# Two output tiles in the attention and a three-tile ring for pre-split weights in a hybrid encoder layer

## The chip, the cores and the metric

The kernel runs on one core of a Trainium2 chip. Its time is that of one execution on the device, in microseconds (us): a median of 1939.59 us over three runs (1938.0 to 1943.59). One further execution was recorded by the hardware profiler; all rows below come from that one.

## The reference, cut to what matters

One layer of an encoder is applied to two sequences, a prompt of 1024 tokens and a sample of 256, each with 16 meta tokens ahead, all in float32.

```
a = rms_norm(h);  p = a @ w_in                    # c_q, c_kv, k_rope and the Hyena input u
s = (q_nope @ k_nope.T + q_rope @ k_rope.T) * scale   # 4 heads, no mask
o_attn = softmax(s) @ v
o_hy   = two gated long convolutions of u (by FFT)
mix = concat(rms_norm(o_attn), rms_norm(o_hy)) @ w_o
h = h + rms_norm(mix)
m = square(relu(rms_norm(h) @ w_ff1)) @ w_ff2     # 1024 -> 4096 -> 1024
h = h + rms_norm(m)
```

## The kernel before

Each float32 product is made of three faster ones (`mm3`, lines 261 to 263): both factors are split into a rounded high part and the rest, the low part. For a weight piece (128 x 512, 256 KB) the high part is a cast on ACT (line 269) and the low part a subtraction, mostly on POOL (line 272); `ring` (line 391) does this for each piece that is streamed.

Phase B computes the attention. It runs over 40 units, 4 heads by 10 tiles of 128 queries: 8 tiles of the prompt and 2 of the sample. In the last head the two sample tiles come first, so units 30 and 31 are the sample's and 32 to 39 the prompt's. In the loop's step i, PE computes the scores of unit i (`softmax`, into the PSUM tile `sset0` or `sset1`), then transposes the probabilities of unit i-1 (`turn`: eight blocks, and a ninth at line 1032, the "last transpose" of a unit), and weights the values of a pair of units (`weigh`, line 1038, into the PSUM tile `po`). At the end of `weigh` ACT copies the transposed reciprocals of the softmax sums from PSUM to `rb` (line 1053), DVE multiplies `po` with `rb` into `ot` (line 1055), and SP's queue stores `ot` to DRAM (line 1056, `oa<-ot`). `rb` and `ot` have one tile each. The scores' ninth block holds 16 keys and 112 columns that POOL sets to zero (line 1005, `MEMSET prob`).

Beside the attention POOL prepares weights of the later sample path (`presplit`, line 363): the first 80 pieces of that path (16 of the output projection, then `w_ff1` and `w_ff2` in turn). A piece is loaded into a tile `pre_raw` (line 372), cast into `pre_hi` (line 384), the cast is subtracted in place (line 272), and the low part is stored to DRAM (line 377, `lo_w_...`). There are four tiles `pre_raw`; a load into one must wait until the store out of it has landed. The load of piece k+2 is written behind the split of piece k and the store of piece k-1. The loop calls `presplit` two times in odd steps and three times in even ones, and runs it to its end before step 33. There the convolution of the sample's Hyena part (`hyena_sample`, line 1469) begins; it loads its input `zs` (line 1478) on SP's queue, PE transposes 16 columns of each of its four parts (line 1441) and then its blocks (line 1495), and its work is woven into the remaining steps.

Later, beside the prompt's Hyena convolution, the sample's output projection and MLP run as filler (`sample_path`). For a pre-split piece `ring` loads the raw weight and the stored low part (lines 398 and 399); for others POOL subtracts (lines 406 and 272). The ring there has four tiles.

What sets the order: within a step the instructions of PE, ACT and DVE are pinned in the written order (`pin`), except the convolution's; everything else is ordered by a scheduler by priority and by its own estimate of when inputs are ready. On the chip each engine's queue and SP's DMA queue run strictly in the order that results.

Of the kernel before, what the change touches and what calls it, by code (L numbers as in the profile page):

```python
# [13 lines left out]
F32 = mybir.dt.float32  # L14
# [7 lines left out]
P = 128  # L22
# [156 lines left out]
def mk(ap, dims):  # L179
    return bass.AP(tensor=ap.tensor, offset=ap.offset, ap=[ap.ap[0]] + [list(d) for d in dims])  # L180
# [54 lines left out]
class Builder:  # L235
# [127 lines left out]
    def presplit(self, pool, n):  # L363
        nc = self.nc
        keys = list(self.sample_pieces())[:n]
        raws = {}

        def load(k):
            if k < n:
                raw = raws[k] = pool.tile([P, 512], F32, name="pre_raw", bufs=4)  # L370
                src = self.piece(*keys[k])
                nc.sync.dma_start(raw.rearrange("p (a b) -> p a b", a=4) if len(src.shape) == 3 else raw, src)

        def store(k):
            if k in raws:
                d = self.d_lo[keys[k]] = self.dr.tile([P, 512], F32, name="lo_" + "_".join(map(str, keys[k])))
                nc.sync.dma_start(d, raws.pop(k))

        load(0)
        load(1)  # L380
        yield
        for k in range(n):
            t = pool.tile([P, 512], F32R, name="pre_hi", bufs=1)
            nc.gpsimd.tensor_copy(t, raws[k])
            self.lo(raws[k], raws[k], t, nc.gpsimd)
            store(k - 1)
            load(k + 2)
            yield
        store(n - 1)
# [514 lines left out]
    def phase_b(self):  # L904
# [4 lines left out]
        with ExitStack() as st:  # L909
# [5 lines left out]
            wk = self.pool(st, "b_work", 2)  # L915
# [122 lines left out]
            def weigh(h, t, qp, pth, ptl, rcs):  # L1038
                vh, vl = t[4:]
                nb, b0 = (8, 0) if qp < 4 else (2, 8)  # L1040
                po = pv.tile([P, 512], F32, name="po", bufs=1)
                o = po[:, :256]
                for b in range(nb):
                    if b == nb // 2:
                        yield
                    self.mm3(o, vh[:, b0 + b], vl[:, b0 + b], pth[:, b], ptl[:, b], b == 0, False)
                b = 8 if qp < 4 else 10
                self.mm3(o, vh[:, b], vl[:, b], pth[:, 8], ptl[:, 8], False, True)
                for i in range(2):
                    nc.tensor.transpose(po[:, 256 + i * 128:384 + i * 128], mk(rcs[i], [[0, 128]]), self.ident)  # L1050
                yield
                rb = wk.tile([P, 256], F32, name="rb", bufs=1)
                nc.scalar.copy(rb, po[:, 256:])
                ot = wk.tile([P, 256], F32, name="ot", bufs=1)
                self.tt(ot, o, rb, ALU.mult)
                (nc.gpsimd if h >= self.dbg.get("oq", 4) else nc.sync).dma_start(self.d_oa[h][:, qp * 256:qp * 256 + 256], ot)
                yield
# [4 lines left out]
            with self.hp(4):  # L1062
                self.hi(krh[0:64], self.ka[0:64])
                self.lo(krl[0:64], self.ka[0:64], krh[0:64])
                raw, rk = stage(TM), stage(T)
                nc.sync.dma_start(rk[64:128], self.ka[0:64])
                nc.sync.dma_start(raw[64:128], self.qr[0:64])
                self.hi(krh[64:128], rk[64:128])
                self.lo(krl[64:128], rk[64:128], krh[64:128])
                self.hi(qst[0][0:64], self.qr[0:64])  # L1070
                self.hi(qst[0][64:128], raw[64:128])
                self.lo(qst[0][64:128], raw[64:128], qst[0][64:128])
                self.ropes.close()
                hps.append(self.pool(st, "b_head1"))
                pre_st = st.enter_context(ExitStack())
                pre = self.presplit(self.pool(pre_st, "b_pre"), 80)
                next(pre)
                for _ in range(self.dbg.get("n6", 6)):
                    next(prep, None)
# [20 lines left out]
            for i in range(n + 3):  # L1100
# [34 lines left out]
                if i >= 3 and i % 2 == 1:  # L1135
                    h, qt = units[i - 3]
                    weighing = weigh(h, heads[h], qt // 2, *pts.pop((i - 3) // 2))
# [781 lines left out]
```

## Time and profile before

| | |
|---|---|
| median of three runs | 1939.59 us |
| profiled execution, its own time | 1943.15 us |
| its span | 1941.4 us |
| PE busy | 1775.0 us (91%), 9806 matmuls |
| DVE busy | 1149.4 us (59%) |
| ACT busy | 751.6 us (39%) |
| POOL busy | 689.2 us (36%) |
| chain that ended last | PE 64%, DVE 15%, DMA 9%, issue 4%, POOL 4%, ACT 4% |

The chain follows the last instruction back, at each step to what released it. A line such as `x <-DMA y` after an idle time names what ended it. SPq is SP's queue of DMA issues. The attention stage lies from about 380 to 685 us, the prompt's convolution with the sample's filler from 685 to 945 us.

### The profile page before, as it was taken

The page shows a single profiled execution, that of the slowest core. Times are in us where ns is not written, and L with a number is a line of the kernel's source. Part 1 is how long each engine was busy: PE and PEld are TensorE (multiplying, and loading weights), DVE is VectorE, ACT ScalarE, POOL GpSimd, SP SyncE. Part 2 cuts the span into 40 slices and gives each one's busy share as a digit, 9 for nine tenths or more (in the row PEclk, how much of TensorE's full clock was granted, in tenths as well). Part 3 has the DMA queues.
Part 4 walks back from the last instruction along what each step waited for, and adds up shares of the span by engine and source line. Part 5 has one row for each costly group of instructions (what it writes and reads, how often), then busy time and mean ns, then how long its engine had stood idle before and what let it go on. Part 6 is the DMA issues. An engine that isn't in the chain of part 4 may idle for free.

```text
span 1941.4 us, 26719 instructions
## 1 busy us (share of the span) xinstructions
PE 1775.0 (91%) x9806; PEld 1561.1 (80%) x9806; DVE 1149.4 (59%) x1862; ACT 751.6 (39%) x1362; POOL 689.2 (36%) x660
## 2 busy tenths in 40 slices
PE   7999999887878988998899799899999999999996
PEld 6899999787778777887779678777888888888885
DVE  6588875753446868999642956763333334333347
ACT  6344443443334454332344565544322222222232
POOL 2112113377882210222376743234422222222234
PEclk9899999988999998999899899999999999999997
DMA  4454535367776276767543574345211111111104
GB/s 165 141 177 159 169 111 196 106 202 242 231 246 210 76 255 200 253 222 240 175 139 120 174 233 143 121 130 166 96 45 44 44 44 44 50 52 56 56 5 142
DMA packets 183654, 275.70 MB, mean 142 GB/s; under 512 B 15258, under 2 KB 89952, under 8 KB 183394
## 3 DMA queue, kind: packets, MB, share of 16 engines
q1 hardware_dynamic: 174936, 254.97, 40.3%
q0 software_dynamic: 5872, 17.06, 2.9%
q10 hardware_dynamic: 2714, 1.96, 0.3%
q8 instruction: 77, 1.26, 0.3%
q14 instruction: 55, 0.45, 0.1%
HBM read 210.90 MB, written 60.38 MB: 140 GB/s over the span
## 4 chain that ended last, share of the span: by engine, by line
PE 64%; DVE 15%; DMA 9%; issue 4%; POOL 4%; ACT 4%; SPq 0%; POOLq 0%; ACTq 0%; DVEq 0%
PE p L261 13%; PE p L263 13%; PE p L262 12%; PE pp L261 2%; PE pp L262 2%; PE pp L263 2%; PE ips L1685 2%; PE wps L263 2%; PE wps L261 2%; PE wps L262 2%; DVE bl L275 2%; POOL pre_raw L272 1%; PE dps L1452 1%; DMA w_raw<-in_w_ff 1%; DMA pre_raw<-in_w_ff 1%
## 5 line engine op out<-in xcount | busy, mean ns | idle before, releaser
L272 POOL TENSOR_TENSOR w_lo<-w_raw,w_hi 128x512 fp32r<-128x512 f32 x276 | 383.3, 1400 | 678.7 <-ACT w_hi L269 622.0
L269 ACT CAST w_hi<-w_raw 128x512 fp32r<-128x512 f32 x388 | 237.8, 619 | 441.4 <-PE p L262 293.3
L261 PE MATMUL p<-sh,w_hi 128*128 128x512 f32 (+1 forms) x800 | 284.5, 360 | 11.1 <-DVE acc L275 4.1
L262 PE MATMUL p<-sl,w_hi 128*128 128x512 f32 (+1 forms) x800 | 283.5, 354 | 11.7 <-DVE sl L272 11.6
L261 PE MATMUL p<-a2h,w_hi 128*128 128x512 f32 (+1 forms) x784 | 285.0, 364 | 8.5 <-ACT a2h L282 4.9
L263 PE MATMUL p<-a2h,w_lo 128*128 128x512 f32 (+1 forms) x784 | 282.7, 361 | 8.8 <-DMA w_lo<-lo_w_ff 6.8
L263 PE MATMUL p<-sh,w_lo 128*128 128x512 f32 (+1 forms) x800 | 284.1, 355 | 4.4 <-POOL w_lo L272 4.4
L262 PE MATMUL p<-a2l,w_hi 128*128 128x512 f32 (+1 forms) x784 | 281.1, 359 | 0.1
L275 DVE TENSOR_TENSOR acc<-acc,p 128x512 f32<-128x512 f32 (+1 forms) x284 | 184.8, 656 | 146.4 <-PE p L263 145.9
L261 PEld LDWEIGHTS p<-sh,w_hi 128*128 128x128 f32 x800 | 154.8, 194 | 35.8 <-ACT sh L269 6.2
L262 PEld LDWEIGHTS p<-sl,w_hi 128*128 128x128 f32 x800 | 155.4, 194 | 34.3 <-DVE sl L272 14.2
L263 PEld LDWEIGHTS p<-a2h,w_lo 128*128 128x128 f32 x784 | 153.1, 195 | 32.0 <-DMA w_lo<-lo_w_ff 7.0
L261 PEld LDWEIGHTS p<-a2h,w_hi 128*128 128x128 f32 x784 | 153.5, 196 | 30.7 <-ACT a2h L282 5.9
L263 PEld LDWEIGHTS p<-sh,w_lo 128*128 128x128 f32 x800 | 155.9, 195 | 25.8 <-POOL w_lo L272 5.1
L262 PEld LDWEIGHTS p<-a2l,w_hi 128*128 128x128 f32 x784 | 153.1, 195 | 22.6 <-DVE a2l L278 0.6
L278 DVE SCALAR_TENSOR_TENSOR rl<-p,rs 128x512 f32<-128x512 f32 (+1 forms) x66 | 44.5, 674 | 199.7 <-PE p L263 199.6
L1779 ACT ACTIVATE rl<-rl 128x512 f32<-128x512 f32 (+1 forms) x66 | 40.9, 619 | 235.6 <-DVE rl L278 235.6
L261 PE MATMUL pp<-ah,w_hi 128*128 128x432 f32 x336 | 123.8, 369 | 0.0
L262 PE MATMUL pp<-al,w_hi 128*128 128x432 f32 x336 | 122.6, 365 | 0.0
L263 PE MATMUL pp<-ah,w_lo 128*128 128x432 f32 x336 | 122.3, 364 | 0.0
L269 ACT CAST pth<-sset 128x512 fp32r<-128x512 f32 (+2 forms) x112 | 51.1, 456 | 140.1 <-DVE ptl L272 64.3
L272 POOL TENSOR_TENSOR pre_raw<-pre_raw,pre_hi 128x512 f32<-128x512 f32 x80 | 102.5, 1281 | 5.5
(390 smaller groups left out, 3772.0 us busy)
## 6 DMA issues: line engine op xcount, KB each, us to landing
w_raw<-in_w_ff SPq DMA_DIRECT2D x292, 256.0 KB, 2.8
pre_raw<-in_w_ff SPq DMA_DIRECT2D x64, 256.0 KB, 3.5
lo_w_ff<-pre_raw SPq DMA_DIRECT2D x64, 256.0 KB, 2.7
w_raw<-in_w_o SPq DMA_DIRECT2D x64, 256.0 KB, 3.4
w_lo<-lo_w_ff SPq DMA_DIRECT2D x64, 256.0 KB, 4.1
fct<-in_c_f POOLq DMA_DIRECT2D x32, 384.0 KB, 4.3
w_raw<-in_w_in SPq DMA_DIRECT2D x32, 256.0 KB, 2.9
k<-spec SPq DMA_DIRECT2D x8, 1024.0 KB, 5.1
```

Of the source, the lines that this page charges most:

```text
L261: mm(out, lhsT=ah, rhs=bh, start=start, stop=False)
L262: mm(out, lhsT=ah, rhs=bl, start=False, stop=False)
L263: return mm(out, lhsT=al, rhs=bh, start=False, stop=stop).ins
L269: return self.nc.scalar.copy(out, src).ins
L272: return (eng or self.nc.vector).tensor_tensor(out, src, f(hi), op=ALU.subtract).ins
L275: (eng or self.nc.vector).tensor_tensor(out, a, b, op=op)
L278: (eng or self.nc.vector).scalar_tensor_tensor(out, x, s, y, op0=op0, op1=op1)
L1452: mm(n, lhsT=self.fc[fr // 4][:, fr % 4, i], rhs=zt, start=True, stop=False)
L1685: mm(ps[:, :width], lhsT=w[q][:, ch], rhs=gr[:, e, q, :width], start=i == 0, stop=i == 3)
L1779: nc.scalar.activation(r, r, AF.Square)
```

## The change

`rb` and `ot` lose their `bufs=1` and take the pool's default of two tiles (2 KB more per partition). The ring `pre_raw` has three tiles, not four (2 KB less). 72 pieces are pre-split, not 80: pieces 72 to 79, group 4 of `w_ff1`, go the ordinary way through `ring`.

```diff
         def load(k):
             if k < n:
-                raw = raws[k] = pool.tile([P, 512], F32, name="pre_raw", bufs=4)
+                raw = raws[k] = pool.tile([P, 512], F32, name="pre_raw", bufs=3)
...
                 yield
-                rb = wk.tile([P, 256], F32, name="rb", bufs=1)
+                rb = wk.tile([P, 256], F32, name="rb")
                 nc.scalar.copy(rb, po[:, 256:])
-                ot = wk.tile([P, 256], F32, name="ot", bufs=1)
+                ot = wk.tile([P, 256], F32, name="ot")
                 self.tt(ot, o, rb, ALU.mult)
...
-                pre = self.presplit(self.pool(pre_st, "b_pre"), 80)
+                pre = self.presplit(self.pool(pre_st, "b_pre"), 72)
```

SP's queue where the pre-splitting ends and the sample's convolution begins (`fc`, `g` and `w_raw` are loads of other constants and weights). Before:

```order
L1056 DMA oa_107<-ot 128x256
L377 DMA lo_w_ff_19_0_6331<-pre_raw 128x512
L377 DMA lo_w_ff_19_1_6333<-pre_raw 128x512
L1056 DMA oa_107<-ot 128x256
L1431 DMA fc_6345<-in_c_fn 128x1024
L1431 DMA fc_6346<-in_c_fn 128x1024
L1056 DMA oa_107<-ot 128x256
L1478 DMA zs<-u_80 128x272
L1478 DMA zs<-u_81 128x272
L1478 DMA zs<-u_82 128x272
L1478 DMA zs<-u_83 128x272
```

After, at the same place:

```order
L377 DMA lo_w_ff_2_6_6152<-pre_raw 128x512
L1056 DMA oa_107<-ot 128x256
L398 DMA w_raw<-in_w_o 128x512
L377 DMA lo_w_ff_2_7_6171<-pre_raw 128x512
L399 DMA w_lo<-lo_w_o_0_3958 128x512
L398 DMA w_raw<-in_w_o 128x512
L399 DMA w_lo<-lo_w_o_0_4000 128x512
L1478 DMA zs<-u_80 128x272
L1478 DMA zs<-u_81 128x272
L1478 DMA zs<-u_82 128x272
L1432 DMA g_6291<-in_c_g 128x1088
L1478 DMA zs<-u_83 128x272
```

The loads of `zs` follow the last pre-split store more closely: three issues lie between, and `g` among them; two stores of `ot` and two loads of `fc` that stood between have moved ahead or behind.

PE's queue behind unit 31's last transpose (L1032 into `sset_3762`), with the transposes of `zs` (L1441) and unit 32's transposes (into `sset_3761`). Before:

```order
L1050 MATMUL po<-ident,rc 128x128 x2
L1032 MATMUL sset_3762<-ident,prob 128x128
L1441 MATMUL pv<-ident,zs 16x128 x4
L261 MATMUL sset_3762<-kh,qnh 128x512
L262 MATMUL sset_3762<-kl,qnh 128x512
```

After, from the end of unit 33's scores:

```order
L996 MATMUL sset_3762<-krh,qst_3769 128x272
L997 MATMUL sset_3762<-krl,qst_3769 128x272
L1441 MATMUL pv<-ident,zs 16x128 x3
L1022 MATMUL sset_3761<-ident,prob 128x128 x6
L1441 MATMUL pv<-ident,zs 16x128
L1022 MATMUL sset_3761<-ident,prob 128x128 x2
L261 MATMUL po<-pth,vh 128x256
L262 MATMUL po<-ptl,vh 128x256
L263 MATMUL po<-pth,vl 128x256
L1032 MATMUL sset_3761<-ident,prob 128x128
```

The transposes of `zs` have moved behind the fifteen score matmuls of unit 33, in between the transposes of unit 32.

POOL's queue at the end of the prompt's convolution, where the pieces from 72 on are now split (`bl` and `cpr` are products of the convolution), as a difference:

```order
 L275 TENSOR_TENSOR cpr<-ends,cf 128x256
-L275 TENSOR_TENSOR bl<-xf,kt 128x512 x3
-L275 TENSOR_TENSOR cpr<-ends,cf 128x256
-L272 TENSOR_TENSOR w_lo<-w_raw,w_hi 128x512 x244
+L275 TENSOR_TENSOR bl<-xf,kt 128x512
+L272 TENSOR_TENSOR w_lo<-w_raw,w_hi 128x512
+L275 TENSOR_TENSOR bl<-xf,kt 128x512
+L272 TENSOR_TENSOR w_lo<-w_raw,w_hi 128x512 x3
+L275 TENSOR_TENSOR bl<-xf,kt 128x512
+L272 TENSOR_TENSOR w_lo<-w_raw,w_hi 128x512 x6
+L275 TENSOR_TENSOR cpr<-ends,cf 128x256
+L272 TENSOR_TENSOR w_lo<-w_raw,w_hi 128x512 x242
```

Ten subtractions now stand among the convolution's last products; eight of them are the pieces no longer pre-split. In PE's queue at this place 73 matmuls of that group stand before the convolution's matmuls of line 1685, where there were 16, and 69 matmuls of the sample's MLP between the two norm sums that follow (line 302), where there were 121.

## Rows read from the trace of the kernel before

**Rows 1.** Windows: one stretch, busy us of each engine (instructions), clock, DMA share, GB/s
```profile
388.00:593.00 205.00, 166.74 (x1095) 154.56 (x1095) 94.97 (x176) 79.45 (x176) 166.41 (x194) 0.90 0.69 225
```
**Rows 2.** Waits, 388 to 593 us: total us, times, longest us
```profile
DVE ot L275 <- DMA oa<-ot: 36.4, 8, 6.6
...
PE po L261 <- DVE ot L275: 21.6, 9, 5.2
...
POOL pre_hi L384 <- DMA pre_raw<-in_w_ff: 16.9, 16, 2.9
```
**Rows 3.** Chain that ended last, 480 to 600 us: start us, us, what
```profile
489.19 0.24 PE sset L261
...
491.46 0.14 PE sset L997
...
536.40 0.62 POOL pre_hi L384
...
538.41 2.57 DMA lo_w_ff<-pre_raw
541.00 3.53 DMA pre_raw<-in_w_ff
544.65 0.62 POOL pre_hi L384
...
553.75 0.62 POOL pre_hi L384
```
**Rows 4.** Timeline of POOL: start us, us, instruction [idle before <-releaser]
```profile
400.09 0.19 POOL L1005 MEMSET prob<- 128x112 f32 x1 [5.14 <-PE sset L1032]
...
477.16 0.61 POOL L384 CAST pre_hi<-pre_raw 128x512 fp32r<-128x512 f32 x1
...
479.20 0.61 POOL L384 CAST pre_hi<-pre_raw 128x512 fp32r<-128x512 f32 x1
...
500.59 1.25 POOL L929 CAST qst<-stage 128x1280 fp32r<-128x1280 f32 x1 [1.09 <-DMA stage<-qr]
501.92 2.88 POOL L272 TENSOR_TENSOR qst<-stage,qst 64x1280 fp32r<-64x1280 f32 x1
```
**Rows 5.** Tile pre_raw: ns min/median/max, first and last start
```profile
L384 POOL CAST pre_hi<-pre_raw x80: 607/610/619, 388.3 to 590.8; 128x512 fp32r<-128x512 f32 x80
```
**Rows 6.** Line 372, the loads of pre_raw
```profile
DMA to landing us min/median/max: 2.6/3.6/6.1
```
**Rows 7.** Line 377, the stores out of pre_raw
```profile
DMA to landing us min/median/max: 2.0/2.7/5.8
```
**Rows 8.** Timeline of SP's queue at the stage's end
```profile
592.79 0.32 SPq L377 DMA_DIRECT2D lo_w_ff<-pre_raw  x1
...
600.06 1.83 SPq L1478 DMA_DIRECT2D zs<-u  x4
```
**Rows 9.** Timeline of POOL: first use of zs
```profile
603.09 0.20 POOL L1486 COPY ends<-zs 128x16 f32<-128x16 f32 x1 [2.37 <-DMA zs<-u]
```
**Rows 10.** Timeline of PE at the same place
```profile
605.66 0.27 PE L1032 MATMUL sset<-ident,prob 128*128 128x128 f32 x1
605.77 0.60 PE L1441 MATMUL pv<-ident,zs 128*16 128x128 f32 x4
...
609.98 0.55 PE L1495 MATMUL pv<-ident,zs 128*128 128x128 f32 x3 [0.77 <-DVE zms L272]
...
612.38 0.27 PE L1032 MATMUL sset<-ident,prob 128*128 128x128 f32 x1
```
**Rows 11.** Timeline of POOL after the convolution
```profile
946.00 3.00 POOL L272 TENSOR_TENSOR w_lo<-w_raw,w_hi 128x512 fp32r<-128x512 f32 x2 [21.36 <-ACT w_hi L269]
```
**Rows 12.** Timeline of PE, 900 to 985 us
```profile
919.26 0.58 PE L263 MATMUL p<-a2h,w_lo 128*128 128x256 f32 x1 [6.80 <-DMA w_lo<-lo_w_ff]
...
923.18 2.08 PE L1685 MATMUL ips<-g,bv 128*128 128x256 f32 x4 [0.56 <-DVE bv L275]
```
**Rows 13.** Waits of PE, 880 to 1010 us
```profile
PE nps L302 <- DVE osq L275: 5.8, 2, 5.4
```

## The prediction

> **What bounds the kernel now.** I read the page first (PE is busy 91% of the span, and the chain that ended last is mostly PE's), then one row of the windows for the attention stage, where the change lies. From 388 to 593 us PE is busy 167 of 205 us at a granted clock of 0.90, and POOL 166 [rows 1]; outside it the change touches only one place near 915 us. The waits of that stage come next [rows 2]: PE stood 21.6 us, in nine pieces, before a weighting because DVE's `ot` came late, and DVE was late because it stood 36.4 us for `oa<-ot`, the store that empties the one `ot` tile. That is what two tiles remove. The same view shows POOL short of `pre_raw` by 16.9 us in 16 pieces. Then the chain of waits [rows 3]: from 536 to 554 us it doesn't run through PE but round the ring of pre-split tiles, subtract, store, load, cast. So the stage has two clocks, PE with its single `ot`, and POOL with its ring. The change relaxes the first and shortens the second.
>
> **The ring.** A piece costs POOL 2.04 us when its tile is there (casts at 477.16 and 479.20 [rows 4]); 80 are cast from 388.3 us on [rows 5]. A tile's turn is cast and subtraction, then the store (2.57 us until SP may issue the load into it), then the load (3.53): casts of the same tile stand at 536.40 and 544.65, 8.25 us, and the next pair at 544.65 and 553.75, 9.10 us [rows 3]. With four tiles four pieces, 8.16 us of POOL work, fit into such a turn, so it hardly shows. With three only 6.12 us fit, and POOL waits the rest: the turn T sets the pace, 24 turns for 72 pieces. Beside it lie POOL's wait of 5.14 us for PE at 400 us and three copies of rotary queries of 4.2 us each (500.59 to 504.80) [rows 4], of which a turn's idle time, T less 6.12, hides a part. The last subtraction so ends at 388.3 + 24T + 5.1 + 3 x (4.2 - T + 6.1) = 424.3 + 21T, if T stays over 6.1.
>
> What is T? The low end is the shortest landings, 2.0 us for a store and 2.6 for a load [rows 6, 7]: 2.04 + 4.6 = 6.64 us, end at 563.7. The quickest turn shown, 8.25, gives 597.6. The high end comes from the kernel before by the same sum: 80 pieces are 20 turns of four, 388.3 + 20T + 5.1 + 3 x (4.2 - T + 8.16) = 430.5 + 17T, and their last store was issued at 592.79 [rows 8], so T was 9.55 on average, with all that holds SP's queue up in it; then three tiles end at 624.9. I take T = 9.0, by the 9.10 row and a little under it, because fewer transfers then share the queues: **the last subtraction ends near 613.3 us, 21 us after today's end, though there are eight pieces fewer.**
>
> The Trainium skill, "DMA: Bandwidth & Descriptors" (section Anatomy of one DMA), fits a transfer at 2.0 us plus its bytes over 436 GB/s, on GpSimd's own queue. For 256 KB that is an estimate of 2.6 us, both ways, a turn of 7.24 and an end at 576.3. The trace disagrees for loads on SP's queue, 3.6 us in the median, and agrees for stores, 2.7 [rows 6, 7]; by its figure the ring would hardly bind and the first rival below would come true.
>
> **What waits for the ring's end.** SP's queue is in order, and in the new order the four loads of `zs`, the sample's convolution input, stand behind the last store: store, `w_lo`, `w_raw`, `w_lo`, three `zs`, `g`, the fourth `zs`. Before, they were issued at 600.06 us, 7 us after the last store, four in 1.83 us, 0.45 each [rows 8]; the first had landed at 603.09 [rows 9], 3.0 us later. With eight issues of 0.45 ahead, the fourth lands 3.6 + 3.0 = 6.6 us after the last subtraction: 619.9 us. PE is in order too. Its four small transposes of `zs` ran at 605.77, at once behind unit 31's last transpose [rows 10]. Now the fifteen score matmuls of unit 33 come first, 489.19 to 491.60 us for such a set, 2.4 us [rows 3], and then PE stops until `zs` is there. Behind it are queued unit 32's transposes, the weighting, unit 32's last transpose (612.38 before) and all the rest of the stage; ACT, DVE and POOL wait for those. So the stage ends later by (613.3 + 6.6) - 605.8 - 2.4 = **+11.7 us**, where 2.4 are the scores done ahead. Generally it is the last subtraction less 601.6: -4.0 for T = 8.25, +23.3 for 9.55. The convolution is no cushion: PE already waited 0.77 us for its `zms` at 609.98 [rows 10], so a later start passes through. From the end of the stage on everything follows.
>
> **The second tile of `ot` and `rb`.** The 21.6 us are real PE idle time [rows 2], but what they can give back is capped by what is late next. A unit's last transpose needs the zeroed tail of its probabilities, and those fills stand in POOL's queue among the pieces: unit 32's behind 71 of 72. However quickly PE weighs, it can't pass the ring, and it meets the `zs` transposes at the end. I count the gain at 0 where the ring ends after 601.6 us, up to -21.6 if the ring didn't bind at all. The second `rb` removes no wait that the trace shows: 0.
>
> **Eight pieces not pre-split** (pieces 72 to 79, the up projection's group 4). Their loads, stores and 16.3 us of POOL work leave the stage; that is in the count of turns. Later they come back as eight subtractions on POOL in place of eight loads of `w_lo`. POOL stood idle 21.36 us before 946 [rows 11], which hides them. In their place the order on PE changes: before the convolution's matmuls at 923.18 there are now 73 filler matmuls, not 16. Before, PE stood 6.80 us there for `w_lo` by DMA [rows 12]. That stall ended 4 us before the convolution's input came (0.56 us of wait at 923.18 [rows 12]), so its end gains nothing by itself, but the 57 matmuls brought forward are work that isn't left for later; behind them PE stood 5.8 us for `osq` [rows 13], which more filler on that side also covers. The gain lies between -8 (6.8 and some of the second) and +5: POOL's subtractions now stand between the convolution's products, and three or four of them at 1.5 us (two in 3.00 [rows 11]) could make PE late at 923. I take half the gain, **-4**.
>
> **Sum.** The profiled execution took 1943.15 us, span 1941.4 and 1.75 around it: 1943.15 + 11.7 - 4 = 1950.9. The median of the three runs is 3.56 lower, and 1950.9 - 3.6 is **1947 us**.
>
> **Rivals.**
> Quick ring: T stays at or under 8.25, the last subtraction ends by 597.6, `zs` has landed by 604.2, and PE isn't held. Then the two `ot` tiles count. For it: nothing but latency makes a turn, and traffic in the stage falls by a tenth. Against it: 16 of today's casts of the MLP's pieces already wait for a load with four tiles [rows 2]. The stage gains between 4.0 and half of 21.6; the middle, -7.4, and -4 later give 1943.15 - 11.4 - 3.6 = 1928. It decides where the ring ends before 601.6 us, T = 8.44.
> Cancelling: T is the mean of the two rows, 8.68; the ring ends at 606.6, the stage is 5.0 us later, and the four won near 915 us pay for it: 1943.15 + 5.0 - 4 - 3.6 = 1940.6.
> Clogged queue: SP stands on a load that waits for the store issued just ahead, with `oa` and the next stores behind it. T = 9.55, +23.3, and the later gain fails: 1963.
> That the change does nothing to `ot` can be left out: the wait is for the tile's own store of one pair earlier, and with two tiles it is that of two pairs earlier.
>
> **How the numbers follow.** A difference of 0.3%, 5.8 us, is about what a measurement of this kernel can tell. My forecast, its own range 1942 to 1956, gets 0.44, quick ring 0.21, cancelling 0.25, clogged 0.10. Of the forecast's 0.44 some 0.05 lie within 0.3%. So slower 0.39 + 0.10 = 0.49, the same 0.30, faster 0.21. The range 1929 to 1961 leaves half of the quick ring's chance and most of the clogged queue's outside, under 2 in 10.
>
> **What would show it.** Right: `ot` no longer waits for `oa<-ot`; casts of the same tile 8.5 to 9.5 us apart, with POOL waiting on most third casts; the last pre-split store past 602 us; one PE wait of 5 us or more at the `zs` transposes; PE's 6.8 us before 923 gone. Wrong: a last store before 600 us; or a wait at `zs` and unit 32's last transpose at today's 612 us all the same, which would mean that PE had gained before it what it loses there; or a new wait of PE on `w_lo` by POOL near 915 us, larger than the one removed.

## The result, and the profile after

| | before | after |
|---|---|---|
| time, median (range) of 6 runs, us | 1942.5 (1938.0 to 1948.91) | 1953.92 (1949.52 to 1960.23) |
| profiled execution, its span, us | 1943.15, 1941.4 | 1960.23, 1958.1 |

The ratio is 1.006, 95% interval 1.0035 to 1.0085: 7 to 17 us slower, where 1947 us had been forecast, 7.4 above the median of that time. The profiled execution of the changed kernel is the slowest of its six, 6.3 us above their median, that of before 0.7 above its own. So of the 16.7 us between the two traces, read below, some 5.6 are the executions' own.

To see where it went, follow TensorE's last transpose of each unit of the attention (the instruction at 605.66 and 612.38 in [rows 10]), then the first matmul into `wps` behind the convolution:

| us | unit 0 | 15 | 17 | 25 | 27 | 31 | 32 | 39 | `wps` | end |
|---|---|---|---|---|---|---|---|---|---|---|
| before | 382.49 | 494.29 | 512.76 | 572.57 | 587.96 | 605.66 | 612.38 | 670.20 | 981.16 | 1941.4 |
| after | 386.12 | 484.28 | 513.19 | 557.72 | 584.76 | 599.54 | 623.69 | 682.97 | 999.42 | 1958.1 |
| difference | +3.6 | -10.0 | +0.4 | -14.9 | -3.2 | -6.1 | +11.3 | +12.8 | +18.3 | +16.7 |

The 3.6 us at unit 0 lie ahead of what the change can move, so they are the execution's own: `after_64` and `after_64_dve` below, one program as far as unit 39, are 4 us apart at unit 0, and from there 4 us at unit 25 and 1.5 at unit 39. The rest reads in four pieces. Within a head TensorE gains (18.5 us by unit 25, without the 3.6). Where the next head's queries are split, at units 15 to 17 and 25 to 27 (called the change of head from here on), it gives most of that back, 10.4 and 11.7 us. Between units 31 and 32 it loses 17.4 us at once. Past the attention it loses 3.9 more: 5.5 up to `wps`, of which 1.6 come back behind it.

The stage's row of the windows, beside [rows 1]: the same TensorE, 25 us less GpSimd, less traffic.

```profile
388.00:593.00 205.00, 166.62 (x1142) 155.14 (x1142) 101.31 (x190) 81.73 (x182) 141.56 (x168) 0.89 0.60 197
```

Its waits (total us, times, longest), beside [rows 2]. `ot` is in none of them any more. In its place GpSimd waits for the ring, and ScalarE and TensorE wait for GpSimd:

```profile
POOL pre_hi L384 <- DMA pre_raw<-in_w_ff: 35.7, 21, 3.7
...
ACT prob L1007 <- POOL qst L272: 26.7, 2, 14.3
...
PE sset L1032 <- POOL prob L1005: 18.1, 5, 8.3
```

The second row is the change of head: the unsplit queries of the next head lie in one of the three probability tiles, and ScalarE can't write the next probabilities until GpSimd, whose queue has the pieces ahead, has split them. The third is the zeroed tail of a probability tile, also queued behind pieces.

The ring in GpSimd's timeline (start, duration, [idle before]); three casts, then a stop:

```profile
528.80 0.61 POOL L384 CAST pre_hi<-pre_raw 128x512 fp32r<-128x512 f32 x1 [1.29 <-DMA pre_raw<-in_w_ff]
...
530.86 0.61 POOL L384 CAST pre_hi<-pre_raw 128x512 fp32r<-128x512 f32 x1
...
532.89 0.61 POOL L384 CAST pre_hi<-pre_raw 128x512 fp32r<-128x512 f32 x1
...
537.16 0.61 POOL L384 CAST pre_hi<-pre_raw 128x512 fp32r<-128x512 f32 x1 [2.16 <-DMA pre_raw<-in_w_ff]
...
544.62 0.61 POOL L384 CAST pre_hi<-pre_raw 128x512 fp32r<-128x512 f32 x1 [1.21 <-DMA pre_raw<-in_w_ff]
...
606.01 0.61 POOL L384 CAST pre_hi<-pre_raw 128x512 fp32r<-128x512 f32 x1 [6.72 <-DMA pre_raw<-in_w_ff]
```

A tile's turn is 8.36 and then 7.46 us here. Over all 69 turns it is 7.4 to 15.7 us, 9.1 in the median; those that begin between 513 and 561 us are all under 8.5, and the last three, 13.8 to 15.7, hold a stop of 6.72. SP's queue at that place, beside [rows 8]:

```profile
596.62 0.42 SPq L1431 DMA_DIRECT2D fc<-in_c_fn  x1
597.10 1.62 SPq L372 DMA_DIRECT2D pre_raw<-in_w_ff  x2
...
607.99 0.33 SPq L377 DMA_DIRECT2D lo_w_ff<-pre_raw  x1
...
610.99 0.44 SPq L398 DMA_DIRECT2D w_raw<-in_w_o  x1
613.95 0.32 SPq L377 DMA_DIRECT2D lo_w_ff<-pre_raw  x1
...
616.02 1.27 SPq L1478 DMA_DIRECT2D zs<-u  x3
```

The two loads issued from 597.10 go out beside the convolution's constants (`fc` here, `mc` from GpSimd), and the first keeps GpSimd waiting until 606, close to 9 us after its issue where the median load took 3.1. That the constants slow it was not tried by itself. The next store, 607.99, and all behind it are late by that, and the first `w_raw` of the sample's path leaves only at 610.99. In ScalarE's timeline its cast is the next instruction from 596.3 us on:

```profile
596.04 0.26 ACT L269 CAST pth<-sset 128x128 fp32r<-128x128 f32 x1
614.29 0.62 ACT L269 CAST w_hi<-w_raw 128x512 fp32r<-128x512 f32 x1 [17.99 <-DMA w_raw<-in_w_o]
```

Behind that cast stands ScalarE's cast of unit 31's transposed probabilities; VectorE waits 17.15 us for it, and TensorE, which needs unit 31's PSUM tile for the scores of unit 33, waits for VectorE (beside [rows 10]):

```profile
599.54 0.27 PE L1032 MATMUL sset<-ident,prob 128*128 128x128 f32 x1
617.46 0.80 PE L261 MATMUL sset<-kh,qnh 128*128 128x512 f32 x1 [17.64 <-DVE ptl L272]
...
622.02 0.49 PE L1441 MATMUL pv<-ident,zs 128*16 128x128 f32 x3
...
623.69 0.27 PE L1032 MATMUL sset<-ident,prob 128*128 128x128 f32 x1
```

The stop stands ahead of unit 33's fifteen scores. The transposes of `zs` behind them run at 622.02 without a wait.

The stop has a tail. In the windows (columns as in [rows 1]) no matmul starts for 17.5 us, and the next 4.8 us run at a granted clock of 0.53, near the lower level of 1.2 GHz:

```profile
599.90:617.40 17.50, 0.00 (x0) 0.00 (x0) 0.42 (x1) 1.50 (x3) 6.00 (x9) 0.64 0.83 247
617.40:622.20 4.80, 4.75 (x17) 4.16 (x18) 0.85 (x3) 2.17 (x5) 0.59 (x3) 0.53 0.92 323
```

Fifteen scores take 617.46 to 622.19, 4.7 us, not the 2.4 of [rows 3].

Near 915 us, waits of TensorE from 880 to 1010 us, beside [rows 12, 13]. Two rows of before that are not shown there:

```profile
PE p L263 <- POOL w_lo L272: 4.4, 2, 2.7
...
PE ips L1685 <- DVE bv L275: 0.7, 2, 0.6
```

After, the 6.80 us on a load is gone and `osq` is down to 0.3. The wait for `bv` has grown, those for `w_hi` and `acc` are new, and the one for GpSimd's `w_lo` is about what it was:

```profile
PE ips L1685 <- DVE bv L275: 5.3, 4, 2.9
PE p L263 <- POOL w_lo L272: 4.9, 4, 1.7
PE p L261 <- ACT w_hi L269: 4.4, 3, 2.6
PE p L261 <- DVE acc L275: 1.5, 1, 1.5
...
PE nps L302 <- DVE osq L275: 0.3, 1, 0.3
```

### The profile page after: what moved, and what is told of

Its sections match the earlier page's. It is cut to its first block, busy times and chain, and to the rows that moved or that the text cites. A ratio compares the mean times of both kernels' runs of the same rounds, so it can differ in the third digit from the quotient of the medians.

```text
span 1958.1 us, 26696 instructions
## 1 busy us (share of the span) xinstructions
PE 1779.3 (91%) x9806; PEld 1563.1 (80%) x9806; DVE 1158.6 (59%) x1862; ACT 752.1 (38%) x1362; POOL 689.7 (35%) x652
## 5 line engine op out<-in xcount | busy, mean ns | idle before, releaser
L272 POOL TENSOR_TENSOR w_lo<-w_raw,w_hi 128x512 fp32r<-128x512 f32 x284 | 399.2, 1418 | 676.9 <-ACT w_hi L269 609.8
L263 PEld LDWEIGHTS p<-sh,w_lo 128*128 128x128 f32 x800 | 155.2, 194 | 21.6 <-DMA w_lo<-lo_w_ff 0.8
L272 POOL TENSOR_TENSOR pre_raw<-pre_raw,pre_hi 128x512 f32<-128x512 f32 x72 | 92.3, 1282 | 5.4
```

The costliest lines, as they stand in the source:

```text
L263: return mm(out, lhsT=al, rhs=bh, start=False, stop=stop).ins
L272: return (eng or self.nc.vector).tensor_tensor(out, src, f(hi), op=ALU.subtract).ins
```

## The experiments

The theory: the ring's end sets the loss, through what SP has queued behind it; the second tile gains within a head and is stopped by GpSimd's queue. The rivals: the eight pieces near 915 us are the loss, or the two tiles are. All runs have their ratio to runs of the kernel before on the same chip, with a 95% interval.

### The ring

`r3_72_single` and `r3_80` are the kernel before with the first line, and with 72 or 80 pieces; `after_64` is the changed kernel with the second.

```
-raw = raws[k] = pool.tile([P, 512], F32, name="pre_raw", bufs=4)
+raw = raws[k] = pool.tile([P, 512], F32, name="pre_raw", bufs=3)
...
-pre = self.presplit(self.pool(pre_st, "b_pre"), 72)
+pre = self.presplit(self.pool(pre_st, "b_pre"), 64)
```

> The changed kernel without its two tiles: ring of three, 72 pieces, single rb and ot. Theory (a turn of the three-tile ring sets the end of the pre-split, and what is queued behind its end holds ScalarE and TensorE): last store near 614 us as in the changed kernel, stage end about 10 to 14 us late, 1952 to 1958 us. Rival (the turn was stretched by the quicker attention's stores, and one tile relieves it): last store near 600, 1943 to 1947 us. Rival (the loss comes from the eight pieces no longer pre-split): 1946 us, and the wait before TensorE's step 32 is gone.

> Before with the ring of three alone: 80 pieces, single tiles. Theory (the ring's end sets the stage's end): eight pieces more than r3_72_single are 2.67 turns of 7.5 to 9 us, quicker ones once TensorE stands: last store near 630 us, stage end 16 to 24 us later than r3_72_single, 1966 to 1978 us. Rival (the end of the ring is hidden and the loss is in each turn's stops): 1952 to 1958 us.

> The changed kernel with 64 pieces in its ring of three in place of 72. Theory: the ring ends 2.67 turns earlier, last store near 590 to 595 us, in front of the work queued for TensorE's step 32, so the stop of 17.6 us goes to under 4; stage end 5 to 10 us before that of the kernel before, eight more pieces split near 900 us cost 0 to 4: 1936 to 1944 us. Rival (the pieces not pre-split are what costs): 1956 us or more. Rival (the quicker attention is stopped at the head changes by GpSimd's queue, as in two_tiles): 1944 to 1948 us.

| ring of three | pieces | last store, us | units 31 to 32, us | ratio |
|---|---|---|---|---|
| r3_80 | 80 | 636.50 | 20.7 | 1.0130 (1.0108 to 1.0153) |
| r3_72_single | 72 | 611.79 | 20.6 | 1.0047 (1.0031 to 1.0063) |
| changed kernel | 72 | 613.95 | 24.2 | 1.0060 (1.0035 to 1.0085) |
| after_64 | 64 | 587.12 | 7.0 | 1.0006 (0.9992 to 1.0019) |

The ring with single tiles makes most of the loss, and it goes with the count of pieces, as the theory says. Two pairs differ by the ring's fourth tile alone: `r3_80` and before (1.0130), and `r3_72_single` and `r4_72` below (1.0047 against 0.9992). `r3_80` is 16 us behind `r3_72_single` by the ratios, the low edge of what was expected; their two traces are 9.2 us apart. Its last store comes 25 us later, but its stop between units 31 and 32 isn't longer. SP's queue, ScalarE and TensorE in `r3_80`:

```profile
612.18 0.43 SPq L398 DMA_DIRECT2D w_raw<-in_w_o  x1
...
615.14 0.62 ACT L269 CAST w_hi<-w_raw 128x512 fp32r<-128x512 f32 x1 [18.80 <-DMA w_raw<-in_w_o]
...
616.54 0.80 PE L261 MATMUL sset<-kh,qnh 128*128 128x512 f32 x1 [14.87 <-DVE ptl L272]
...
639.19 1.75 SPq L1478 DMA_DIRECT2D zs<-u  x4
```

So the load of `w_raw` and the loads of `zs` come apart here. The stop ends with the cast of `w_raw`, 23 us before `zs` leaves: it is that load's, and neither the last store's nor `zs`'s. What the later end adds stands behind unit 32, where units 32 to 39 take 70.2 us, 58.6 in `r3_72_single`. In `after_64` the cast finds its load, and TensorE doesn't stop (ScalarE, start, duration, idle before):

```profile
599.25 0.37 ACT L269 CAST pth<-sset 128x256 fp32r<-128x256 f32 x1 [2.61 <-PE sset L1022]
...
604.25 0.63 ACT L269 CAST w_hi<-w_raw 128x512 fp32r<-128x512 f32 x1
```

The order has changed too: unit 31's cast stands ahead of that of `w_raw` here, as in `r4_72`, and behind it in the three other kernels of the table. The scheduler chooses that order, and no run held it fixed. So the runs show what the shorter ring costs with the order that comes with it, and not how the loss divides between the later end and the order.

The stage of `after_64` ends 8.5 us earlier than before's, counted from unit 0 to unit 39 (279.2 against 287.7 us), inside the expected 5 to 10. The time doesn't show it: past unit 39 it loses what it won (below).

### The second tile

`two_tiles` leaves the ring of four and 80 pieces. The copied reciprocals and the weighted values become one tile, multiplied in place, and two of those fit into the bytes of the two single ones. `two_tiles_set` adds the middle line, `two_tiles_off` the next two as well, `two_tiles_free` the last.

```
-rb = wk.tile([P, 256], F32, name="rb", bufs=1)
-nc.scalar.copy(rb, po[:, 256:])
-ot = wk.tile([P, 256], F32, name="ot", bufs=1)
-self.tt(ot, o, rb, ALU.mult)
+ot = wk.tile([P, 256], F32, name="ot")
+nc.scalar.copy(ot, po[:, 256:])
+self.tt(ot, o, ot, ALU.mult)
...
-nc.gpsimd.memset(p[:, nk:nk + 112], 0.0)
+nc.vector.memset(p[:, nk:nk + 112], 0.0)
...
-nc.gpsimd.tensor_copy(qst[h], raw)
-self.lo(qst[h][64:128], raw[64:128], qst[h][64:128], nc.gpsimd)
+nc.scalar.copy(qst[h], raw)
+self.lo(qst[h][64:128], raw[64:128], qst[h][64:128])
...
-nc.sync.dma_start(raw[i * 64:i * 64 + 64], self.d_qr[...])
+nc.scalar.dma_start(raw[i * 64:i * 64 + 64], self.d_qr[...])
```

> Before with the copied reciprocals and the weighted values in one tile (multiplied in place) and two of these tiles, in the bytes of the two single tiles; ring of four tiles and 80 pieces as before. Theory (the two tiles are no loss; the shorter ring is): DVE's 36.4 us of waits for ot's store are gone, TensorE reaches step 31 some 6 to 9 us earlier, as it did in the changed kernel (599.54 against 605.66, from a start 3.2 us later), and with a ring whose last store stands at about 593 it keeps half of it or more: 1933 to 1939 us. Rival (the ring binds, so the two tiles give nothing): within 2 us of before. Rival (the two tiles themselves cost, by another order on the engines): 1946 or more.

Measured 1.0015 (0.9996 to 1.0033): nothing gained, if anything 3 us lost. The expected gain did not come. The two other pairs that differ by the second tile say the same: the changed kernel against `r3_72_single`, 1.0060 and 1.0047, and `two_tiles_72` against `r4_72` below, 1.0009 and 0.9992. The waits of `two_tiles` from 388 to 593 us:

```profile
PE sset L1032 <- POOL prob L1005: 26.2, 10, 5.6
...
ACT prob L1007 <- POOL qst L272: 20.8, 2, 10.5
```

So even with four tiles TensorE only changes what it waits for: 21.6 us for `ot` [rows 2] against 26.2 for the cleared tail, and the queries.

> As two_tiles, with only the clearing of the 112 columns moved from GpSimd to VectorE; the queries' split stays on GpSimd behind the pieces. Theory: the 26.2 us of waits for the clearing go, but the ones at the two head changes grow by about as much (20.8 to 30 or more), since the tile that holds the unsplit queries keeps one of the three probability buffers until GpSimd comes to it: no gain, 1945 to 1950 us. Rival (the clearing alone was the wait): 1936 to 1941 us.

1.0013 (0.9997 to 1.0029). TensorE waits for no cleared tail any more and is 19 us ahead at unit 25 (171.0 us after unit 0, before 190.1), but at the change of head nearly all of it goes, as expected: 19.6 of 23.4 us between units 17 and 19, 16.8 of 18.1 between units 27 and 29. Its waits, 388 to 593 us:

```profile
ACT prob L1007 <- POOL qst L272: 36.4, 2, 18.9
```

> As the run two_tiles (two in-place tiles, ring of four, 80 pieces), and what the attention still asks of GpSimd's queue behind the pre-split is taken off it: the clearing of 112 columns of each probability tile goes to VectorE, the two steps that split the next head's rotated queries to ScalarE and VectorE. Theory (in two_tiles 26.2 us of waits for the clearing and 20.8 us for the queries' tile, both queued behind the pieces, took the place of the 37.1 us for ot's store): both waits are gone, TensorE is 10 to 18 us ahead of before at step 24 and keeps it over the head changes, the stage ends 6 to 15 us earlier: 1930 to 1938 us. Rival (the pre-split's own end, near 590 to 597, holds it again): stage end within 3 us, 1943 to 1947. Rival (VectorE, which gets more work, becomes the bound): 1946 or more.

1.0061 (1.0039 to 1.0083): slower, and the theory's numbers were wrong. The time is the second rival's, but its reason isn't: VectorE itself stands 52.4 us for ScalarE's cast of the queries, 388 to 620 us. ScalarE now reaches the queries' cast itself and stands there, in front of everything else it has to do (timeline of `two_tiles_off`):

```profile
507.27 1.26 ACT L929 CAST qst<-stage 128x1280 fp32r<-128x1280 f32 x1 [23.53 <-DMA stage<-qr]
```

The loads for it leave at 500.80 us, in SP's queue behind stores that wait for GpSimd's subtractions. The queue of GpSimd had been exchanged for that of SP.

> As two_tiles_off (two in-place tiles, clearing on VectorE, the queries' split on ScalarE and VectorE; ring of four, 80 pieces), and the two loads of each next head's unsplit queries are issued by ScalarE instead of by SP, so that they no longer stand behind the pre-split's stores there. Theory (what the two tiles give is taken back by whatever of the next head is queued behind the pieces: in two_tiles_off ScalarE stood 49.5 us in 3 waits on those loads): these waits fall under 10 us, TensorE is 15 to 20 us ahead of before at step 25 and still 8 or more at step 31, stage end 6 to 16 us earlier than in before: ratio 0.992 to 0.997, 1926 to 1936 us. Rival (the stores of the attention, which stay on SP behind the pieces, or the end of the pre-split stop it again): stage end within 4 us of before, 1938 to 1945 us.

1.0029 (1.0015 to 1.0043). Another queue didn't free them. ScalarE stood from 483.3 us to 504.95, and only then issued the loads (timeline of `two_tiles_free`):

```profile
483.00 0.27 ACT L269 CAST pth<-sset 128x128 fp32r<-128x128 f32 x1
504.95 2.90 ACTq L928 DMA_DIRECT2D stage<-qr  x2
514.54 1.26 ACT L929 CAST qst<-stage 128x1280 fp32r<-128x1280 f32 x1 [31.27 <-DMA stage<-qr]
```

In the trace each of these two loads waits for a semaphore, the counter that tells of a landing, on which a store of the pre-split counts up. The first waits for that of the store issued at 502.09 us, which has landed at 504.88, and leaves at 504.95; the second for that of the store issued at 504.35, which has landed at 507.37, and leaves at 507.39. So the loads have left SP's queue and still wait for the pieces.

### The pieces no longer pre-split

`r4_72`, `two_tiles_72` and `two_tiles_free72` are before, `two_tiles` and `two_tiles_free` with this edit; the ring keeps four tiles.

```
-pre = self.presplit(self.pool(pre_st, "b_pre"), 80)
+pre = self.presplit(self.pool(pre_st, "b_pre"), 72)
```

> Before with 72 instead of 80 pre-split pieces, ring of four, single tiles. Theory by the changed kernel's trace (GpSimd's subtractions of the eight pieces between 922 and 951 us stand between the convolution's products and stretch VectorE's beside them): the pre-split ends some 16 us earlier (last store near 577) and gives TensorE 0 to 2 us at most, the eight pieces cost about 3: 1942 to 1947 us. Rival (the prediction's term: eight pieces fewer gain 4 us near 915): 1938 us.

> Two in-place tiles as in the run two_tiles, ring of four, 72 pieces. If two tiles gain 3 to 9 us and the eight pieces cost 3: 1936 to 1942 us. If the end of the pre-split held the quicker TensorE in two_tiles, eight pieces fewer free it: up to 5 us faster than two_tiles. If the eight pieces gain 4 as predicted: 4 us faster than two_tiles.

> As two_tiles_free, with 72 pieces in the ring of four. If the end of the pre-split holds the quicker TensorE in two_tiles_free, eight pieces fewer move it some 16 us forward and give up to 8 us; if not, the eight pieces split later cost 0 to 4 us (r4_72 against before: ratio 0.9992; two_tiles_72 against two_tiles: 0.9994): between 8 us faster and 4 us slower than two_tiles_free, likeliest 1 us faster.

Ratios: `r4_72` 0.9992 (0.9973 to 1.0012); `two_tiles_72` 1.0009 (0.9989 to 1.0029), beside 1.0015 with 80; `two_tiles_free72` 1.0004 (0.9990 to 1.0019), beside 1.0029. The interval of `r4_72` reaches from 5 us faster to 2 slower, so it can't tell its theory (0 to 5 us slower) from its rival (4 faster). `two_tiles_72` shows none of the gain that was expected of the two tiles. The last is 5 us faster than its partner: up to unit 39 it wins 8.2 us, with its last store at 561 and not at 579 us. From unit 39 to the end, by the traces, 72 pieces against 80 gave +3.9 us in the changed kernel against before and -4.6, +0.4 and +2.6 in these three; `r3_72_single` against `r3_80` is a fifth pair, +2.3. That is nothing that a sign can be put to, where the prediction had -4. Divided at `wps` it reads better. Up to it the eight pieces cost 5.5, 2.6, 5.6 and 2.9 us in four of the pairs and won 1.2 in `r4_72`; behind it they won 0.7 to 3.4 us in all five. The work moves: in the changed kernel's trace some 43 more matmuls stand between unit 39 and `wps`, and 43 fewer behind it.

`after_64_dve` takes up the loss that `after_64` has there. The 16 pieces it no longer pre-splits are subtracted on VectorE:

```
+self.late = list(self.sample_pieces())[n:80]
...
-eng = nc.vector if every and self.count % every == 0 else nc.gpsimd
+eng = nc.vector if key in self.late or every and self.count % every == 0 else nc.gpsimd
```

> As after_64, with the subtractions of the 16 pieces that before pre-split and after_64 does not moved from GpSimd to VectorE. Theory (GpSimd's subtractions stand between the convolution's products and stretch VectorE's beside them: 128x512 products 0.68 us alone, 1.7 us beside them, and TensorE waits 12.9 us for bv): TensorE's wait for bv falls under 5 us, and the time is 3 to 7 us under that of after_64: ratio to before 0.997 to 0.999. Rival (VectorE is the tighter engine there, and 16 subtractions more on it cost as much): ratio 1.000 to 1.004.

0.9966 (0.9949 to 0.9983), faster than both kernels. From unit 39 to `wps` it takes 310.9 us; `after_64` 323.7, before 311.0. Of the 12.8 us between the two runs 3.7 come back behind `wps`, where `after_64` has less left to do; 9.1 stay. VectorE's products in before and, below, in `after_64`, 890 to 965 us, by shapes (xcount | busy us, mean ns):

```profile
L275 DVE TENSOR_TENSOR bl<-xf,kt 128x512 f32<-128x512 f32 x12 | 10.2, 873 | 0.5 <-DMA kt<-k 0.5
...
L275 DVE TENSOR_TENSOR bl<-xf,kt 128x512 f32<-128x512 f32 x12 | 13.5, 1146 | 0.0
```

In `after_64_dve`, the same (its lines stand one to two further down):

```profile
L273 DVE TENSOR_TENSOR w_lo<-w_raw,w_hi 128x512 fp32r<-128x512 f32 x16 | 11.5, 729 | 3.0 <-ACT w_hi L270 3.0
L276 DVE TENSOR_TENSOR bl<-xf,kt 128x512 f32<-128x512 f32 x11 | 7.1, 677 | 0.0
```

The expected fall of TensorE's wait for `bv` under 5 us came only to 5.8, and a wait for VectorE's subtractions is new. In `after_64` and, below, in `after_64_dve`, 880 to 1010 us:

```profile
PE ips L1685 <- DVE bv L275: 12.9, 5, 5.5
...
PE p L264 <- DVE w_lo L273: 5.9, 3, 3.4
PE ips L1687 <- DVE bv L276: 5.8, 2, 5.6
```

`combined64` puts together what paid: two in-place tiles, the clearing on VectorE, ring of four, 64 pieces, 16 subtractions on VectorE.

> Before with what paid so far put together: two in-place tiles, the clearing on VectorE, a ring of four with 64 pieces, and the 16 pieces no longer pre-split subtracted on VectorE when they are used. Theory (the quicker attention needs GpSimd's queue short at the head changes, and the late pieces need GpSimd out of the convolution's way): the waits behind GpSimd's queue at the two head changes (36.4 us in two_tiles_set) fall under 25, stage end at or before that of after_64, TensorE has no wait over 3 us for bv near 900: ratio 0.992 to 0.996, 1926 to 1936 us. Rival (the head changes come with the pieces whatever the ring, since fewer pieces are spread over fewer units): as after_64_dve, ratio 0.996 to 0.999, 1936 to 1941 us.

0.9928 (0.9914 to 0.9941), 1927.2 us: the fastest here. The stage takes 268.4 us from unit 0 to unit 39, 19 less than before. Its waits from 388 to 620 us:

```profile
ACT prob L1009 <- POOL qst L273: 20.1, 1, 20.1
```

One of the two changes of head is free; the other still costs TensorE 19.4 us. That TensorE has no wait over 3 us for `bv` did not come true: the longest is 5.6. How the gain divides among its four edits (ring of four is as before) was not tried.

## Why the prediction was right, step by step

The time is in the range and the change goes the way that was forecast. Of the steps behind it the ring's end held, its consequence held in size and not in kind, and the gain near 915 us did not come. In the sum's terms the prediction had +11.7 - 4 = 7.7 us; the traces have +9.1 for the stage, from unit 0 to unit 39, and +3.9 past it.

**The wait for `ot`** is gone, as said, and the second `rb` shows nowhere.

**The ring's end** was forecast at 613.3 us, the last store came at 613.95, in an execution whose first cast was 3.3 us later (391.54). Put into the prediction's sum, T was 8.9. The size was right partly by luck. The stop of 6.72 us at the end was not foreseen, and without it the same sum ends near 607; turns under 8.5 in the middle made up for turns of 10 us and more at the start and at the changes of head. The two rows on which T rested, 8.25 and 9.10, are turns of four tiles, which hold 8.16 us of GpSimd's own work, so they could not show how quick a turn of three can be: the quickest here took 7.4. Loads landed in 3.1 us in the median and stores in 2.5 (3.6 and 2.7 in [rows 6, 7]). The Trainium skill, "DMA: Bandwidth & Descriptors" (section Anatomy of one DMA), whose figure gave an estimate of 2.6 us each way, fits these stores and comes nearer to these loads; its turn of 7.24 is under every turn of this trace.

**What waits for it.** The step said: TensorE does unit 33's scores and then stops at the transposes of `zs`, 11.7 us. The kind of wait was wrong. TensorE stops 17.64 us ahead of those scores, for ScalarE's cast of the first `w_raw`, whose load sits in SP's queue one place ahead of the last store; the wait at `zs` that was named as a sign of being right isn't there. `r3_80` shows that cast to stop TensorE by itself. The last `zs` had its first use on GpSimd at 622.68 (619.9 forecast), so in the changed kernel `zs` would have held TensorE to about the same time. That is argued from the order, which no run held fixed. The size came out near because both loads stand beside the ring's end in one queue, not because the step named the right one. From unit 0 to unit 39 the stage lost 9.1 us.

**The second tile, 0.** Right in the sum, and in the reason only for a part. As the step said, the stop swallows what TensorE is ahead when it comes to it: 9.8 us early at unit 31, 7.7 late at unit 32 (both without the 3.6 of unit 0). But the step had the ring's end as the only thing that caps the gain, and with a ring of four tiles GpSimd's queue takes it all the same (`two_tiles`, `two_tiles_72`). The stage of `after_64`, whose ring of three ends early, keeps 8.5 us; how much of that the second tile gives is open, as no run has its ring with single tiles. Of what GpSimd's queue holds up, the fills that the prediction named are one half; the queries of the next head, which it had only as work in the count of turns, are the other.

**Eight pieces, -4.** This term failed, within its bounds of -8 and +5: +3.9 us in the changed kernel's trace, and by five pairs no gain that can be told from none. The two stalls went as said, and work did move ahead, which gives 0.7 to 3.4 us back behind `wps`. But GpSimd's subtractions came between the convolution's products, the risk named (the 21.36 us of idle time in which the step hid them lie behind those products), and did more than queue: VectorE's products beside them took longer. `after_64` and `after_64_dve` show it with 16 pieces: 9.1 us from unit 39 to the end.

**The rivals.** Quick ring needed an end before 601.6 us; with three tiles only the rings of 64 pieces have that, eight fewer than in the change, and with VectorE doing the late subtractions it is a gain. Cancelling needed the -4, which didn't come. Clogged queue had the right place, SP at the stage's end, and too long a turn.

## What to carry to other kernels

Before adding a double buffer, look through every in-order queue (the helper engine's, and the DMA queue whose stores wait for that engine) for what the freed engine needs from behind the slow work: it moves only as far as that. A prefetch ring that loses a tile should lose items too, until it ends before the first load that must follow it. Work that is no longer done ahead should come back where it doesn't slow the engine beside it, and that is found by the mean time of one instruction, not by idle time.

## What the runs showed of the hardware

- VectorE's products of two 128x512 tiles take 0.68 us, and up to 1.78 while GpSimd subtracts 128x512 tiles (mean 1.15 against 0.68 above); beside GpSimd's own products it is up to 1.75 (mean 0.87 in before). The Trainium skill, "SBUF — State Buffer" (section SBUF: two separate sides), says that the two engines lock a shared pair of ports for a whole instruction when VectorE has two SBUF inputs and GpSimd reads SBUF. The trace agrees in that both get slower (in `after_64_dve` GpSimd's subtraction takes 1.3 us while VectorE is idle and 1.7 in the median beside it); that the lock lasts a whole instruction no run here shows. The same subtraction takes 0.73 us on VectorE, and 1.58 on GpSimd in `after_64` (x22, 890 to 965 us).
- A load issued by ScalarE can wait for transfers of SP's queue: in `two_tiles_free` two of them left 0.07 and 0.02 us after stores of the pre-split had landed, 21.7 us after ScalarE had come to them.
- After 17.5 us with no matmul TensorE was granted 0.53 of its clock for 4.8 us, and 1.00 again from 622.2 us. The stop so cost some 2.3 us more than it lasted.
- With 197 GB/s in the stage, not 225, the median load of a piece landed in 3.1 us, not 3.6. That the one is the cause of the other was not tried; `r4_72`, with a ring of four and 209 GB/s, still has 3.6.
